# A ragged self-attention on one core: new step orders and PSUM banks for seven loops, and 64-row pairs in the two-tile loops

## The chip, the core and the metric

The kernel runs on one core of one Trainium2 chip. The metric is the device time of one execution in microseconds (us), as the median of several executions. Beside the timed executions one execution is recorded by the hardware profiler; its time is a little longer than the span of its trace, since some work lies around the first and the last instruction.

## What is computed

32 sequences of 64 to 511 rows (of 512 possible) and 512 columns in fp32 are each projected to queries, keys and values, attended with 8 heads of 64, and written back; rows beyond a sequence's length are zero.

```python
for b in range(batch):
    x_b = x[b, :lengths[b]]
    q, k, v = np.split(x_b @ w_qkv, 3, axis=-1)          # 512 x 1536 weights
    # reshape to 8 heads of 64
    scores = q @ k.T / sqrt(64)
    attn = softmax(scores)
    output[b, :lengths[b]] = attn @ v
```

The lengths are data. The program sorts the sequences by length on the chip.

## The kernel before

**Loops by length.** After sorting, the sequences are processed in 16 pairs, in order of falling length. `LOOPS` (line 220) holds twelve padded lengths N: 512, 448, 384, 352, 320, 288, 256, 224, 192, 160, 128 and 96. For each there is a loop whose body handles one pair in two *positions*, j = 0 and 1. A loop runs as often as the lengths ask; with this draw 1, 1, 1, 3, 1, 1, 1, 2, 1, 2, 1 and 1 times. A sequence of length N has n tiles of 128 rows: four for 512 and 448, three for 384 to 288, two for 256 to 160, one for 128 and 96. "Shared" loops (448, 320, 288, 192, 160) put the last half tiles of both sequences into one.

**What a position does.** In a position, the scores of sequence j are computed, exponentiated and multiplied with its values, while the queries, keys and values of the next sequence, o = 1 − j, are projected. So the projection in the last position of a loop is already for the first sequence of the next loop; the division of the results of a loop's last sequence is still running on VectorE when the next loop begins. The steps, which `position` (line 994) turns into instructions, are:

- S: scores (line 1174) of a group of heads, 64-row matmuls into two PSUM banks; ScalarE (ACT) exponentiates them from there (line 1192).
- A: attention times values (line 1336), 128-row matmuls of 65 columns into one bank; VectorE (DVE) takes the reciprocal of the sum (R, line 1348), multiplies in which rows live (U, line 1354), and divides into `out_nat` (O, line 1357).
- B: queries and keys of the next sequence as pairs of 64-row matmuls into two banks (`half_qk`, lines 1248 and 1222). The pair's two halves go to different banks at once; the second part, with the halves turned, adds the rest. U is the same for the values of two tiles (`half_values`, line 1267). The copies out of PSUM are lines 1255 and 1274.
- K and Q: the same by 128-row matmuls, one bank (`project`, line 275, copies at line 1294). V: values of one tile (line 286, copy at line 1310). W: values of a shared last tile (line 1128).
- L: a column of ones for rows that live (DVE, line 1093); P: the mask (DVE, line 1017) and the casts to fp16 (GpSimd, line 346); X: transposes of the next x by DMA on SyncE's queue (line 303); D: loading a later x, clearing tails, on the same queue.

**What sets the order.** `ORDER` (line 222) is a list of steps for each loop and position. "S0@67" is step S0 with banks 6 and 7. "B0a@50 ... B0b:da" is the first and the second part of B0; the second names the engines for its two copies, d for DVE and a for ACT. A star puts a copy on ACT. A loop whose list has no "@" gets its banks from `allotted` (line 959), a ring that gives the bank unused for longest. In the kernel before, 256, 224, 192, 160, 128 and 96 have no "@".

**Waits.** Each engine runs its instructions in the order of the list. Where an instruction needs a bank or buffer that another engine still holds, `plan_waits` (line 38) adds a semaphore wait. Loops can be entered from several others, so `by_rank` (line 1456) names every operation of a kind by how many of its kind follow in the position: O0 is the position's last division. A wait on a name is a wait on the operation of that rank, in whichever loop came before.

Of the kernel before, what the change touches and what calls it, by code (L numbers as in the profile page):

```python
# [162 lines left out]
def kernel(  # L163
# [25 lines left out]
    def ring(n, shape, dtype, name, pool=const):  # L189
# [804 lines left out]
    def position(N, j, at, ring):  # L994
# [213 lines left out]
        def halves(name, blocks, widths, copies, outs):  # L1208

            ks = ring.pop(0)

            def matmuls(turned):
                count = len(blocks[0])
                for m in range(count):
                    for c in range(NC):
                        for half in range(2):
                            z = half ^ turned
                            lhs, rhs = blocks[z][m]  # L1220
                            rows = slice(HD * half, HD * (half + 1))
                            last = nc.tensor.matmul(  # L1222
                                banks[ks[z]][:, m * widths : (m + 1) * widths],
                                lhs(rows, c),
                                rhs(rows, c),
                                start=(m == 0 and c == 0 and not turned),
                                stop=(c == NC - 1 and bool(turned)),
                            )
                return last

            held = (f"bk{ks[0]}", f"bk{ks[1]}")

            begun = ("b" if name[0] == "B" else "u") + name[1]

            def first():
                op(begun, "PE", lambda: matmuls(0), (f"xT{o}",), held)

            def second(engines):
                op(("q" if name[0] == "B" else "v") + name[1], "PE", lambda: matmuls(1), (f"xT{o}",), held, after=begun)
                for z in range(2):  # L1240
                    by_act, bank = engines[z] == "a", banks[ks[z]]
                    copy = lambda z=z, by_act=by_act, bank=bank: copies[z](copy_on(by_act), bank)
                    op(outs[z][0], "ACT" if by_act else "DVE", copy, (f"bk{ks[z]}",), outs[z][1])

            first()
            return second

        def half_qk(name, x):
# [5 lines left out]
            def into(buf):  # L1254
# [7 lines left out]
                (f"{up}{x}", tuple(f"{what}{o}.{x * gm + m}" for m in range(gm)))  # L1262
# [121 lines left out]
        for step in steps(N, j):  # L1384
            step = step.split("@")[0]
            kind, act = step[0], step.endswith("*")
            if kind in "BU":
                name, engines = step[:2], step[4:]
                if engines:
                    opened.pop(name)(engines)  # L1390
                else:
                    opened[name] = (half_qk if kind == "B" else half_values)(name, int(name[1]))
                continue
# [62 lines left out]
    def by_rank(ops):  # L1456


        kinds = {"bu": "b", "kqv": "g", "KQV": "G", "a": "a", "O": "O", "s": "s", "S": "S"}
# [249 lines left out]
```

## Time and profile before

| | us |
|---|---|
| median of 3 runs | 339.42 (339.03 to 340.7) |
| profiled execution | 340.88 |
| span of its trace | 339.0 |

| engine | busy us | share of the span |
|---|---|---|
| TensorE (PE) matmuls | 320.6 | 95% |
| ScalarE (ACT) | 260.4 | 77% |
| VectorE (DVE) | 213.8 | 63% |
| GpSimd (POOL) | 103.8 | 31% |

The loops begin, by their first matmul, at these times in the trace (us): 512 at 22.8, 448 at 60.2, 384 at 96.0, 352 at 121.4, 320 at 194.6, 288 at 217.1, 256 at 241.9, 224 at 257.1, 192 at 285.0, 160 at 298.2, 128 at 320.9, 96 at 327.6.

The busy share of an engine is a mean over all of these. The view that is used most is the timeline of one engine: each row has the start of a group of like instructions, the time from its first start to its last end, the engine, the line of the kernel, the operation, output and inputs, the shape, the count, and in brackets the idle time before it with what ended it. "<-issue" is idle time that ended with nothing the profile shows. The ends of matmuls are modelled, so rows of PE overlap by some tenths of a microsecond; the difference between the starts of two groups is the measure of what the first cost. Rows of the windows give the busy time of each engine in a stretch and the granted TensorE clock, 1.00 for full speed.

### The profile page before, as it was taken

The page shows a single profiled execution, that of the slowest core. Times are in us where ns is not written, and L with a number is a line of the kernel's source. Part 1 is how long each engine was busy: PE and PEld are TensorE (multiplying, and loading weights), DVE is VectorE, ACT ScalarE, POOL GpSimd, SP SyncE. Part 2 cuts the span into 40 slices and gives each one's busy share as a digit, 9 for nine tenths or more (in the row PEclk, how much of TensorE's full clock was granted, in tenths as well). Part 3 has the DMA queues.
Part 4 walks back from the last instruction along what each step waited for, and adds up shares of the span by engine and source line. Part 5 has one row for each costly group of instructions (what it writes and reads, how often), then busy time and mean ns, then how long its engine had stood idle before and what let it go on. Part 6 is the DMA issues. An engine that isn't in the chain of part 4 may idle for free.

```text
span 339.0 us, 12004 instructions
## 1 busy us (share of the span) xinstructions
PE 320.6 (95%) x4472; PEld 203.4 (60%) x4472; DVE 213.8 (63%) x675; ACT 260.4 (77%) x395; POOL 103.8 (31%) x149
## 2 busy tenths in 40 slices
PE   7989999899999989999999999799999999989891
PEld 5444536455556546556656656666668776868670
DVE  6555656676675556566475556657776665777774
ACT  5379899698968878978978898577667768877751
POOL 6546040504030330330232143043222224444231
PEclk9999999999999999999999999989999999999997
DMA  6974994463629957947948748979836865696771
GB/s 219 390 264 94 336 218 134 155 251 80 226 56 277 324 110 256 262 142 276 300 139 281 229 141 323 257 217 291 224 128 186 210 209 172 151 275 201 240 194 73
DMA packets 72127, 72.13 MB, mean 213 GB/s; under 512 B 41872, under 2 KB 41872, under 8 KB 72080
## 3 DMA queue, kind: packets, MB, share of 16 engines
q1 hardware_dynamic: 72032, 71.52, 70.5%
q8 instruction: 27, 0.44, 0.6%
q14 instruction: 20, 0.16, 0.2%
q10 hardware_dynamic: 48, 0.00, 0.0%
HBM read 28.32 MB, written 33.55 MB: 183 GB/s over the span
## 4 chain that ended last, share of the span: by engine, by line
PE 87%; DVE 5%; DMA 2%; issue 2%; ACT 1%; SPq 0%; POOL 0%; DVEq 0%; ACTq 0%; POOLq 0%
PE banks L1222 33%; PE banks L1336 15%; PE banks L1174 14%; PE banks L275 13%; PE banks L286 9%; DVE out_nat L1357 2%; PE banks L1128 2%; DMA x_nat<-in_x_dram 1%; DMA xT<-x 1%; DVE rcp L1354 1%; DVE rcp L1348 1%; PE banks L746 0%; ACT et L1192 0%; DVE kT L795 0%; SPq L623 0%
## 5 line engine op out<-in xcount | busy, mean ns | idle before, releaser
L1192 ACT ACTIVATE et<-banks 128x704 f16<-128x704 f32 (+7 forms) x260 | 201.6, 824 | 39.9 <-PE banks L1174 37.8
L346 POOL TENSOR_TENSOR x<-x_nat,mask 128x512 f16<-128x512 f32 x85 | 86.3, 1041 | 188.0 <-DVE mask L1017 158.9
L1222 PE MATMUL banks<-xT,w_r 64*128 64x352 f16 (+5 forms) x1024 | 102.5, 324 | 3.0 <-DVE out_nat L1357 3.0
L1174 PE MATMUL banks<-qz,kT 64*128 64x352 f16 (+11 forms) x640 | 76.5, 297 | 4.5 <-DVE out_nat L1357 1.4
L1336 PEld LDWEIGHTS banks<-v_aug,et 128*128 128x128 f16 x1792 | 62.0, 98 | 18.3 <-issue 8.3
L1222 PEld LDWEIGHTS banks<-xT,w_r 64*128 64x128 f16 x1024 | 47.1, 95 | 40.7 <-PE banks L1222 10.4
L1336 PE MATMUL banks<-v_aug,et 128*128 128x65 f16 x1792 | 69.2, 194 | 0.7 <-ACT et L1192 0.7
L1357 DVE TENSOR_TENSOR out_nat<-banks,rcp 128x256 f32<-128x256 f32 (+1 forms) x136 | 64.1, 471 | 5.4 <-DMA out_dram<-out_nat 0.8
L275 PE MATMUL banks<-xT,w_r 128*128 128x160 f16 (+6 forms) x512 | 51.4, 252 | 0.8 <-DMA xT<-x 0.5
L1174 PEld LDWEIGHTS banks<-qz,kT 64*128 64x128 f16 x640 | 27.6, 94 | 30.8 <-issue 8.0
L1255 DVE CAST qz<-banks 128x352 f16<-128x352 f32 (+5 forms) x41 | 22.6, 551 | 36.6 <-PE banks L1222 36.2
L275 PEld LDWEIGHTS banks<-xT,w_r 128*128 128x128 f16 x512 | 39.5, 98 | 7.4 <-issue 1.5
L286 PE MATMUL banks<-w_r,xT 128*128 128x512 f16 x156 | 39.3, 379 | 0.5 <-DVE xT L755 0.5
L1348 DVE RECIPROCAL rcp<-banks 128x4 f32<-128x4 f32 (+1 forms) x136 | 24.7, 181 | 19.6 <-PE banks L1336 18.3
L1222 PE MATMUL banks<-w_r,xT 64*128 64x512 f16 x256 | 33.0, 376 | 0.2 <-issue 0.2
L1274 DVE CAST v_aug<-banks 128x512 f16<-128x512 f32 x24 | 15.9, 690 | 17.5 <-PE banks L1222 17.5
L1255 DVE CAST kT<-banks 128x352 f16<-128x352 f32 (+5 forms) x41 | 22.1, 548 | 7.0 <-PE banks L1222 7.0
L1354 DVE TENSOR_TENSOR rcp<-rcp,v_aug 128x4 f32<-128x4 f32 (+1 forms) x108 | 20.4, 189 | 3.7
L1310 ACT CAST v_aug<-banks 128x512 f16<-128x512 f32 x21 | 12.5, 595 | 11.0 <-PE banks L286 11.0
L286 PEld LDWEIGHTS banks<-w_r,xT 128*128 128x128 f16 x156 | 12.9, 97 | 13.2 <-ACT et L1192 1.1
L1222 PEld LDWEIGHTS banks<-w_r,xT 64*128 64x128 f16 x256 | 12.2, 94 | 10.6 <-PE banks L1222 1.0
L1294 ACT CAST kT<-banks 128x320 f16<-128x320 f32 (+3 forms) x17 | 8.4, 491 | 7.2 <-PE banks L275 7.2
(91 smaller groups left out, 154.3 us busy)
## 6 DMA issues: line engine op xcount, KB each, us to landing
x_nat<-in_x_dram SPq DMA_DIRECT2D x12, 768.0 KB, 5.4
out_dram<-out_nat SPq DMA_DIRECT2D x12, 768.0 KB, 4.0
x_nat<-in_x_dram SPq DMA_DIRECT2D x14, 512.0 KB, 3.9
x_nat<-in_x_dram SPq DMA_DIRECT2D x7, 1024.0 KB, 6.6
out_dram<-zeros SPq DMA_DIRECT2D x12, 512.0 KB, 5.4
out_dram<-out_nat SPq DMA_DIRECT2D x12, 512.0 KB, 4.4
out_dram<-out_nat SPq DMA_DIRECT2D x4, 1024.0 KB, 4.6
out_dram<-zeros SPq DMA_DIRECT2D x12, 256.0 KB, 5.4
```

Source lines behind the costliest of these rows:

```text
L275: last = nc.tensor.matmul(dst[:, 0:N], w_r[:, c, w0 : w0 + P], xT[:, c, 0:N], start=(c == 0), stop=(c == NC - 1),)
L286: last = nc.tensor.matmul(pv, xT[:, c, t * P : (t + 1) * P], w_r[:, c, 2 * D : 3 * D], start=(c == 0), stop=(c == NC - 1),)
L346: return engine.tensor_tensor(out=x16, in0=x32, in1=live.broadcast_to([P, D]), op=ALU.mult)
L1174: last = nc.tensor.matmul(psc[par][:, x * wide : x * wide + N], kT[r, i, c0 : c0 + P], qz[r, i, 0:N], start=True, stop=True,)
L1192: return nc.scalar.activation(out=et[:, :, x0:x1, 0:N], in_=got.rearrange("p j (x q) -> p j x q", q=wide)[:, :, x0:x1, 0:N], func=AF.Exp, ...
L1222: last = nc.tensor.matmul(banks[ks[z]][:, m * widths : (m + 1) * widths], lhs(rows, c), rhs(rows, c), start=(m == 0 and c == 0 and not tur ...
L1255: return lambda copy, bank: copy(out=buf[:, ms, 0:N], in_=bank[:, 0 : gm * N].rearrange("p (m q) -> p m q", q=N),)
L1274: return lambda copy, bank: copy(out=v_bufs[o][:, t, :, 0:HD], in_=bank.rearrange("p (h d) -> p h d", d=HD))
L1336: last = nc.tensor.matmul(pav[:, g, qt, :], e_bufs[e][:, c0 + qt * P : c0 + (qt + 1) * P], v_aug[:, kt, h, :], start=(kt == 0), stop=(kt = ...
L1348: return nc.vector.reciprocal(out=rcp, in_=pav[:, :, :, HD])
L1354: return nc.vector.tensor_tensor(out=rcp, in0=rcp, in1=rows, op=ALU.mult)
L1357: return nc.vector.tensor_tensor(out=o_t[:, 0:n, h0 * HD : (h0 + heads) * HD].rearrange("p t (g d) -> p g t d", d=HD), in0=pav[:, :, :, 0:HD],
```

## The change

`ORDER` has new lists for 512, 384, 352, 320, 256, 224 and 192, of which 352's differ in a few banks and in the order of four steps; the lists of 448, 288, 160, 128 and 96 are the same. In 256, 224 and 192, banks are now written out, and 128-row K, Q (and in 256 and 224 V) steps are replaced by 64-row pairs. For that `halves` can place two blocks of the output in each of its two banks. Where two blocks go to a bank (N up to 256), the work of a B is in three parts, a, b and c: block 0 of both banks with the halves straight; block 0 with the halves turned and block 1 turned; block 1 straight. The copies, one for each bank with both blocks, follow the last part. Each part waits for the part before it. The names of first and middle parts now carry the kind, number and part, and `by_rank` files the u parts with the other last ones. A queries' or keys' copy of two blocks is `into` as before with a width of 2N. 

```diff
     ORDER = {
-        512: "L P D S0@67 U1a@34 S1@01 S2@67 U1b:dd S3@12 B0a@50 S4@67 B0b:da S5@23 B3a@14 S6@67 B2a@05 S7@23 "
-        "B2b:dd S8@67 B3b:ad A0@0 S9@23 S10@67 A1@5 A2@4 A3@1 S11@23 U0a@05 S12@67 U0b:dd S13@34 A4@1 "
-        "S14@67 B1a@20 S15@45 B1b:aa A5@6 A6@5 X A7@3 | L P D S0@12 U1a@47 S1@56 U1b:da S2@12 B3a@30 "
-        "S3@45 B3b:dd S4@12 U0a@76 S5@45 U0b:dd S6@01 B1a@23 S7@45 B1b:ad S8@67 S9@01 A0@4 B2a@23 S10@67 "
-        "B2b:dd S11@45 B0a@10 S12@67 B0b:dd S13@45 S14@23 A1@6 A2@7 S15@45 A3@1 A4@3 A5@0 A6@2 X A7@5",
+        512: "L P D S0@56 S1@23 U1a@74 S2@56 U1b:dd S3@01 B1a@32 S4@67 B1b:dd S5@45 S6@01 A0@6 A1@3 S7@45 "
+        "B0a@27 S8@01 B0b:dd S9@34 B2a@65 S10@12 B2b:ad U0a@74 S11@23 S12@56 U0b:ad S13@01 A2@3 A3@2 A4@4 "
+        "S14@56 B3a@37 S15@12 B3b:ad A5@4 A6@5 X A7@7 | L P D S0@23 U0a@10 S1@56 U0b:ad S2@23 U1a@47 "
+        "S3@01 B1a@56 S4@23 B1b:da S5@01 U1b:dd S6@23 B2a@56 S7@01 B2b:ad S8@34 B3a@72 S9@01 A0@5 A1@6 "
+        "S10@34 B3b:dd S11@01 S12@56 A2@3 A3@4 S13@12 B0a@07 S14@56 A4@3 S15@12 B0b:da A5@3 A6@1 X A7@0",
         448: "L P D S0@67 B2a@32 S1@45 B2b:da S2@67 B1a@10 S3@23 B1b:dd S4@67 B0a@54 S5@23 B0b:dd S6@01 S7@67 "
...
-        384: "L P D U0a@32 S0@45 S1@67 U0b:dd S2@01 B1a@54 S3@67 B1b:dd S4@23 B2a@10 S5@67 B2b:dd S6@23 S7@45 "
-        "A0@6 A2@7 S8@01 B3a@32 S9@56 B3b:aa B0a@10 S10@45 B0b:ad S11@23 V2*@6 A4@0 X A6@2 | L P D S0@67 "
-        "B3a@43 S1@01 B3b:dd S2@67 B2a@52 S3@01 B2b:dd S4@34 S5@67 V2@1 A0@2 S6@45 B1a@73 S7@01 B1b:aa "
-        "A2@2 S8@01 S9@45 U0a@67 B0a@32 S10@01 S11@45 B0b:da U0b:da A4@0 X A6@1",
-        352: "L P D V2@4 S0@56 S1@01 U0a@27 S2@56 S3@34 U0b:dd S4@01 B2a@65 S5@34 B2b:dd S6@01 A0@2 A2@7 S7@01 "
-        "B0a@56 S8@34 B0b:ad B1a@10 S9@34 B3a@27 S10@56 B1b:dd S11@34 B3b:aa A4@6 X A6@3 | L P D S0@01 "
-        "B2a@42 S1@67 B2b:da S2@01 B0a@53 S3@67 B1a@42 S4@01 B1b:dd S5@67 B0b:ad S6@01 A0@4 S7@67 U0a@25 "
-        "S8@01 S9@34 U0b:ad B3a@10 S10@67 S11@34 B3b:aa A2@5 A4@7 A6@3 V2*@6 X",
-        320: "L P D S0@45 U0a@10 S1@67 S2@45 U0b:da B1a@76 S3@45 B1b:ad S4@23 A0@0 S5@45 B0a@67 S6@23 B0b:ad "
-        "S7@45 B3a@10 S8@67 B3b:da S9@45 B2a@32 S10@67 S11@01 B2b:da A2@5 A4@4 X A6@7 | L P S0@23 S1@01 "
-        "W0@6 D B0a@32 S2@01 B0b:da S3@45 B2a@76 S4@01 S5@23 B2b:dd U0a@45 S6@01 S7@23 U0b:da B1a@76 "
-        "S8@01 B3a@32 S9@45 B1b:da B3b:dd S10@01 S11@45 A0@7 A2@6 A4@3 X A6@2",
+        384: "L P D S0@56 B3a@34 S1@12 B3b:ad S2@56 B2a@07 S3@23 B1a@14 S4@56 B2b:ad S5@23 B1b:dd S6@56 B0a@70 "
+        "S7@12 B0b:dd S8@34 U0a@65 S9@12 S10@34 U0b:ad S11@12 A0@0 A2@7 A4@6 V2*@3 X A6@0 | L P D S0@12 "
+        "B1a@47 S1@56 B1b:ad S2@01 B2a@32 S3@56 B3a@74 S4@01 B2b:da S5@56 B3b:da U0a@03 S6@12 S7@67 "
+        "U0b:da B0a@54 S8@12 S9@67 A0@0 A2@3 S10@12 B0b:da S11@67 A4@0 V2*@2 X A6@7",
+        352: "L P D V2@4 S0@56 S1@01 U0a@27 S2@56 S3@34 U0b:dd S4@01 B2a@65 S5@34 B2b:dd S6@01 A0@7 A2@2 S7@01 "
+        "B0a@56 S8@34 B0b:aa B1a@10 S9@34 B3a@27 S10@56 B1b:dd S11@34 B3b:aa A4@6 X A6@3 | L P D S0@01 "
+        "B0a@42 S1@67 B0b:da S2@01 B2a@53 S3@67 B1a@42 S4@01 B1b:dd S5@67 B2b:ad S6@01 A0@4 S7@67 U0a@25 "
+        "S8@01 S9@34 U0b:ad B3a@10 S10@67 S11@34 B3b:aa A2@5 A4@7 V2*@6 X A6@3",
+        320: "L P D S0@12 B2a@45 S1@67 B2b:ad S2@23 U0a@01 S3@67 S4@45 U0b:da B0a@67 S5@34 B1a@25 S6@01 B0b:dd "
+        "S7@34 B1b:ad S8@01 A0@6 S9@23 B3a@57 S10@01 B3b:dd S11@23 A2@4 A4@6 X A6@5 | L P S0@23 S1@01 "
+        "W0@4 D B1a@76 S2@01 B2a@32 B1b:ad S3@01 B2b:dd S4@45 A0@6 S5@01 B0a@73 B3a@24 S6@01 B0b:dd S7@56 "
+        "B3b:ad A2@1 S8@67 S9@23 U0a@54 S10@67 S11@01 U0b:da A4@3 X A6@0",
         288: "L P D S0@45 B2a@72 B3a@36 S1@45 B2b:da B3b:dd S2@45 S3@01 U0a@27 S4@56 S5@34 U0b:dd S6@01 B0a@56 "
...
-        256: "L P V0 V1 S0 S1 K2 Q0 S2 S3 A0 K0* A2 A4 Q2* X D A6",
-        224: "L P K0 K2* S0 S1 Q0* Q2 S2 S3 A0 A2 V1* A4 V0* X D A6",
-        192: "L P V0* S0 S1 Q0 K0* S2 S3 A0 K2* A2 A4 Q2* X D A6 | L P K0* S0 S1 W0 V0 S2 S3 A0 Q0* A2 A4 K2* "
-        "Q2* X D A6",
+        256: "L P U0a@23 S0@45 U0b:da B1a@10 S1@67 B0a@54 S2@23 B0b S3@67 B1b B0c:aa A0@3 A2@2 A4@7 A6@6 "
+        "B1c:aa X D | L P U0a@34 S0@12 U0b:ad B0a@05 S1@67 B1a@21 B0b S2@34 S3@67 B0c:da B1b A0@3 B1c:aa "
+        "X D A2@4 A4@7 A6@6",
+        224: "L P B0a@30 S0@12 B0b B1a@54 B0c:da S1@67 B1b S2@01 U0a@23 S3@67 B1c:dd U0b:aa X D A0@1 A2@0 A4@7 "
+        "A6@4 | L P B1a@65 S0@23 B1b B0a@01 B1c:ad B0b S1@23 S2@67 B0c:dd U0a@45 A0@3 A2@0 S3@12 U0b:aa X "
+        "D A4@7 A6@6",
+        192: "L P B1a@01 B0a@23 S0@45 B1b S1@67 B0b B1c:da S2@45 B0c:dd S3@67 A0@1 V0*@0 X D A2@2 A4@3 A6@5 | "
+        "L P W0@4 B0a@60 S0@12 B0b B1a@37 B0c:dd S1@12 B1b S2@45 A0@6 S3@12 B1c:aa A2@0 A4@5 V0*@4 X D "
+        "A6@6",
         160: "L P S0 S1 S2 K0 Q2* A0 Q0* A2 K2* A4 V0* X D A6 | L P S0 S1 S2 W0 Q0 K0* A0 Q2* A2 K2* A4 V0* X "
...
-        def halves(name, blocks, widths, copies, outs):
+        def halves(name, blocks, width, copies, outs):
...
-            def matmuls(turned):
-                count = len(blocks[0])
-                for m in range(count):
+            def matmuls(parts):
+                for m, turned, opens in parts:
                     for c in range(NC):
...
-                                start=(m == 0 and c == 0 and not turned),
-                                stop=(c == NC - 1 and bool(turned)),
+                                start=(c == 0 and opens),
+                                stop=(c == NC - 1 and not opens),
...
+            todo = [[(0, 0, True)], [(0, 1, False)]]
+            if len(blocks[0]) == 2:
+                todo[1].append((1, 1, True))
+                todo.append([(1, 0, False)])
+            begun = []
+            def go_on(engines):
+                k, parts = len(begun), todo[len(begun)]
+                last = k == len(todo) - 1
+                title = "qu"[name[0] == "U"] + name[1] if last else f"b{'BU'.index(name[0])}{name[1]}{k}"
+                op(title, "PE", lambda: matmuls(parts), (f"xT{o}",), held, after=begun[-1] if begun else "")
+                begun.append(title)
+                for z in range(2 if last else 0):
...
+            return go_on
...
-        kinds = {"bu": "b", "kqv": "g", "KQV": "G", "a": "a", "O": "O", "s": "s", "S": "S"}
+        kinds = {"b": "b", "kqvu": "g", "KQV": "G", "a": "a", "O": "O", "s": "s", "S": "S"}
```

More of the change, by code (lines that the diff above doesn't have):

```diff
@@ L1222, in matmuls @@
                             last = nc.tensor.matmul(
-                                banks[ks[z]][:, m * widths : (m + 1) * widths],
+                                banks[ks[z]][:, m * width : (m + 1) * width],
                                 lhs(rows, c),
                                 rhs(rows, c),
-                                start=(m == 0 and c == 0 and not turned),
-                                stop=(c == NC - 1 and bool(turned)),
+                                start=(c == 0 and opens),
+                                stop=(c == NC - 1 and not opens),
                             )
@@ L1231, in halves @@
             held = (f"bk{ks[0]}", f"bk{ks[1]}")
[L1233 to L1240, printed above, removed]
+            todo = [[(0, 0, True)], [(0, 1, False)]]
[7 more added lines that the diff above has]
+                title = "qu"[name[0] == "U"] + name[1] if last else f"b{'BU'.index(name[0])}{name[1]}{k}"
+                op(
+                    title,
+                    "PE",
+                    lambda: matmuls(parts),
+                    (f"xT{o}",),
+                    held,
+                    after=begun[-1] if begun else "",
+                )
+                begun.append(title)
+                for z in range(2 if last else 0):
                     by_act, bank = engines[z] == "a", banks[ks[z]]
@@ L1243, in second @@
                     op(outs[z][0], "ACT" if by_act else "DVE", copy, (f"bk{ks[z]}",), outs[z][1])
-            first()
-            return second
+            return go_on
         def half_qk(name, x):
@@ L1261, in half_qk @@
             outs = [
-                (f"{up}{x}", tuple(f"{what}{o}.{x * gm + m}" for m in range(gm)))
+                (f"{up}{x * gm}", tuple(f"{what}{o}.{x * gm + m}" for m in range(gm)))
                 for up, what in (("Q", "qz"), ("K", "kT"))
@@ L1388, in position @@
                 name, engines = step[:2], step[4:]
-                if engines:
-                    opened.pop(name)(engines)
-                else:
+                if name not in opened:
                     opened[name] = (half_qk if kind == "B" else half_values)(name, int(name[1]))
+                opened[name](engines)
                 continue
```

## The prediction

> **What bounds the kernel now.** I read the page first, then TensorE's timeline for places where it stood idle, then VectorE's timeline at the same places.
>
> ```profile
> span 339.0 us, 12004 instructions
> ...
> PE 320.6 (95%) x4472; PEld 203.4 (60%) x4472; DVE 213.8 (63%) x675; ACT 260.4 (77%) x395; POOL 103.8 (31%) x149
> ...
> PE 87%; DVE 5%; DMA 2%; issue 2%; ACT 1%; SPq 0%; POOL 0%; DVEq 0%; ACTq 0%; POOLq 0%
> ```
>
> TensorE is busy for 95% of the span and carries 87% of the chain of waits. The change removes no matmul work, so it can gain only what PE loses: its idle time, its slowed time, and its changes between 64-row and 128-row matmuls. The rows below are PE's timeline at the borders ("seams") between loops, and within loop 352; the bracket is idle time and its releaser.
>
> ```profile
> 60.20 0.36 PE L1174 MATMUL banks<-qz,kT 64*128 64x448 f16 x2
> 61.80 0.74 PE L1222 MATMUL banks<-xT,w_r 64*128 64x448 f16 x6 [1.23 <-DVE out_nat L1357]
> ...
> 96.02 1.04 PE L1222 MATMUL banks<-w_r,xT 64*128 64x512 f16 x8 [0.22 <-issue]
> ...
> 121.42 1.03 PE L286 MATMUL banks<-w_r,xT 128*128 128x512 f16 x4
> 122.38 0.32 PE L1174 MATMUL banks<-qz,kT 64*128 64x352 f16 x2
> 122.98 0.32 PE L1174 MATMUL banks<-qz,kT 64*128 64x352 f16 x2 [0.27 <-DVE out_nat L1357]
> 123.14 1.03 PE L1222 MATMUL banks<-w_r,xT 64*128 64x512 f16 x8
> 124.00 0.31 PE L1174 MATMUL banks<-qz,kT 64*128 64x352 f16 x2
> 125.05 0.32 PE L1174 MATMUL banks<-qz,kT 64*128 64x352 f16 x2 [0.74 <-DVE v_aug L1310]
> ...
> 195.63 0.70 PE L1174 MATMUL banks<-qz,kT 64*128 64x320 f16 x4
> 196.17 0.60 PE L1222 MATMUL banks<-w_r,xT 64*128 64x512 f16 x4
> ...
> 217.13 0.30 PE L1174 MATMUL banks<-qz,kT 64*128 64x288 f16 x2
> 219.24 2.10 PE L1222 MATMUL banks<-xT,w_r 64*128 64x288 f16 x16 [1.81 <-DVE out_nat L1357]
> 221.11 0.47 PE L1174 MATMUL banks<-qz,kT 64*128 64x288 f16 x2
> 221.35 1.78 PE L1222 MATMUL banks<-xT,w_r 64*128 64x288 f16 x16
> ...
> 296.70 0.41 PE L1336 MATMUL banks<-v_aug,et 128*128 128x65 f16 x8
> 298.19 0.73 PE L1174 MATMUL banks<-qz,kT 64*128 64x160 f16 x16 [1.08 <-ACT qz L1294]
> ```
>
> VectorE at the same seams, with the clock of the fourth (the window's columns: length; PE, PEld, DVE, ACT, POOL busy; granted clock; DMA share; GB/s):
>
> ```profile
> 61.23 0.42 DVE L1357 TENSOR_TENSOR out_nat<-banks,rcp 128x256 f32<-128x256 f32 x1
> ...
> 124.07 0.26 DVE L1093 TENSOR_SCALAR v_aug<-alive 128x24 f16 x1 [1.15 <-issue]
> ...
> 124.31 0.68 DVE L1310 CAST v_aug<-banks 128x512 f16<-128x512 f32 x1
> ...
> 218.54 0.56 DVE L1357 TENSOR_TENSOR out_nat<-banks,rcp 128x384 f32<-128x384 f32 x1
> 220.43 0.20 DVE L1093 TENSOR_SCALAR v_aug<-alive 128x16 f16 x1 [1.33 <-issue]
> ...
> 297.56 0.42 DVE L1357 TENSOR_TENSOR out_nat<-banks,rcp 128x256 f32<-128x256 f32 x1
> ...
> 219.24:222.60 3.36, 3.36 (x30) 2.45 (x32) 0.50 (x4) 0.67 (x2) 1.61 (x2) 0.50 1.20 281
> ```
>
> Three things are to be seen. First, a new loop's first projection waits for a bank whose last division (L1357) is still queued on DVE: PE starts at 61.80, 0.15 us after the division that ends at 61.65, and at 219.24, 0.14 us after 219.10. That 0.15 is the release latency. Second, on entering loops 352 and 288 DVE stands for 1.15 and 1.33 us "<-issue" at the first instruction of the new code (L1093), with nothing to wait for. The V copy at 124.31 is late by that, and S3 at 125.05 by the copy. Third, after 1.81 us of idle PE runs at half clock until 222.6.
>
> **The change, part by part.** Against the profiled execution: 340.88 us, the 339.0 of its span and 1.9 around it.
>
> *320 to 288.* Old: 320 ends with A6@2 and 288 begins with S0, B2a@72, so B2a waits for the very last division. From 217.13 two S matmuls take 0.12 (sixteen of that width take 0.98, below), so B2a is 1.99 late. The slowed stretch is 3.36 us at half clock, so 1.7 more is lost: 3.7 in all. New: 320 ends with S11@01 U0b:da A4@3 X A6@0. B2a@72 needs the exps of S9 and S10, B3a@36 the division of A4 and an exp: all before A6's. What is late next: S0@45 needs both V copies of U0b (one 0.69 on DVE, one 0.6 on ACT), with A4 and A6 (18 AV matmuls each, 1.1 us in all) between, and I take 0.25. S3@01 needs A6's division, which has the two B parts (about 2 us) to hide in. U0a@27 needs Q2's copy, which stands on DVE behind L and M, hence behind the 1.33 us entry stall if it stays: I take 1.0. The instruction stream of DVE keeps its length within 0.3% (770 for 772), so I let both stalls stay. −3.7 + 0.25 + 1.0 = **−2.4**; −3.5 if the stall goes.
>
> *512 to 448.* Old: S0, B2a@32 with bank 2 held by the last but one division. 61.80 − 60.20, less 0.20 for two matmuls (0.16 at 352 columns, 122.98 to 123.14), is 1.40 lost. New: 512 ends A5@3 A6@1 X A7@0, so B2a needs the last but two, a whole A6 and A7 earlier. Its Q2 copy is then behind L and M on DVE, in front of S3@23: I take 0.2 for that. **−1.2**.
>
> *384 to 352.* Lost: 122.98 − 122.38 less 0.15, and 125.05 − 124.00 less 0.15: 1.35. New: 384 ends V2*@2 X A6@7 instead of A4@0 X A6@1. S1@01 now needs exps and A4; that is 0.45 gained. The 0.9 at S3@34 hangs on the V2@4 copy behind the stall, and the steps of 352 there are unchanged. **−0.45**; −1.3 if the stall goes, 0 if another bank binds.
>
> *192 to 160.* S0 of 160 waits for the last division: 298.19 − 296.70, less 0.24 for eight AV matmuls (269.69 to 269.93, below), is 1.25, of which 0.1 is the row change below. 160 keeps its own banks, and 192's written-out ones change what its first two held last. Then S2 waits for V0's ACT copy and K0 for A6: I take 0.45. **−0.8**.
>
> *Three small seams* (448 to 384, 352 to 320, 288 to 256). The rows at 96.02 (0.22) and 195.63 (0.54 until 196.17 for four S, where twice 0.16 would do even at 352 columns) show two; I take the third, which shows no idle row, at half of one. **−0.55**.
>
> *Row changes and parts.* A switch between 64 and 128 rows, and the cost of a second part:
>
> ```profile
> 268.83 1.03 PE L286 MATMUL banks<-w_r,xT 128*128 128x512 f16 x4
> 269.69 0.41 PE L1336 MATMUL banks<-v_aug,et 128*128 128x65 f16 x8
> 269.93 0.38 PE L286 MATMUL banks<-w_r,xT 128*128 128x512 f16 x1
> ...
> 153.02 0.32 PE L1174 MATMUL banks<-qz,kT 64*128 64x352 f16 x2
> 153.18 0.76 PE L1222 MATMUL banks<-xT,w_r 64*128 64x352 f16 x8
> 153.78 0.31 PE L1174 MATMUL banks<-qz,kT 64*128 64x352 f16 x2
> 154.00 1.37 PE L1222 MATMUL banks<-xT,w_r 64*128 64x352 f16 x16
> ...
> 233.01 1.14 PE L1222 MATMUL banks<-xT,w_r 64*128 64x288 f16 x16
> 233.99 0.28 PE L1174 MATMUL banks<-qz,kT 64*128 64x288 f16 x2
> ```
>
> Four 128-row matmuls of 512 take 0.86 (268.83 to 269.69), with a switch to 64 rows after them 0.96 (121.42 to 122.38), and eight 64-row ones 0.86 (123.14 to 124.00). So a pair costs what one 128-row matmul does, and a **switch costs 0.10**. A second part one S behind its first starts 0.22 after the S (153.78 to 154.00) instead of 0.16 (153.02 to 153.18): 0.06 for each such place. Counted along the steps, 384 loses 4 switches and 4 such places: **−0.65**. 320 gains 4 switches, loses 2 places, and puts more copies on ACT in between, which I take at 0.2: **+0.4**. The eight positions' pairs in 256, 224 and 192 are narrower than any that the trace has; at 288 columns sixteen matmuls, eight pairs, take 0.98 (233.01 to 233.99), 122.5 ns a pair, where 288/512 of 215 would be 121. Some 320 pairs at 0 to 1.5 ns more: I take +0.3. They lose 8 switches (−0.8) and gain 4 places where a part waits (+0.2). **−0.3** for the three together.
>
> *Rank names and copies at 256, 224, 192.* A wait names an operation by its rank from the end of a position, so 224's B0a@30 on entry waits for 256's A2 division too, and its first S for the copies after part c; 192's S0@45 waits for V1's copy on ACT. The nearest row to each wait is one ACT copy (0.595, below) and its bounds are 0 and that plus 0.15. I take **+0.5** for both.
>
> ```profile
> 22.80:60.20 37.40, 37.36 (x512) 19.40 (x513) 21.28 (x62) 33.88 (x38) 12.83 (x14) 1.00 0.72 196
> ...
> 241.90:257.13 15.23, 15.14 (x177) 10.74 (x178) 11.98 (x37) 9.60 (x12) 4.29 (x5) 1.00 0.57 153
> ...
> L1192 ACT ACTIVATE et<-banks 128x1024 f16<-128x1024 f32 x40 | 39.1, 1031 | 8.6 <-PE banks L1174 8.0
> ...
> L1274 ACT CAST v_aug<-banks 128x512 f16<-128x512 f32 x8 | 4.8, 595 | 0.0
> ```
>
> *512 itself.* ACT is busy 33.88 of 37.40 us. The new order has four copies on ACT in its second position where the old has two (and three for four in the first): 16 × 1.03 + 4 × 0.595 = 18.9 of 18.7 us, so an S may wait for a late exp. Bounds 0 and one copy, 0.6; I take **+0.4**.
>
> X and D (SP's transposes and loads) move by one A or two at most and no wait names SP at these seams, so I cost them at nothing; their cover is the whole position, and 0.2 would be lost where it is gone.
>
> Sum: −2.4 −1.2 −0.45 −0.8 −0.55 −0.65 +0.4 −0.3 +0.5 +0.4 = **−5.05**. Profiled: 335.8. The median shown is 1.46 below the profiled execution, so the forecast is **334.4 us**; the bounds of the single terms put it between 332.3 and 336.5.
>
> One rule speaks against the new pairs. The Trainium skill, "TensorEngine Tiling (Array Packing)", section "Gotcha 1: PSUM Pressure", says that different row tiles write to different PSUM banks. Here a B of a two-tile loop holds two banks through three parts, where a 128-row projection held one; no row of this trace has three parts.
>
> **Rivals.**
> 1. *Copies bunch in the two-tile loops, and it gets slower.* Nothing is copied until part c; then two blocks wide copies come at once ("B0c:aa", "B1c:aa"). In the first position of 256 ACT would have four exps and five copies: 4 × 1.03 + 5 × 0.595 = 7.1 of 7.6 us (half of 15.23). If each of the eight positions of 256, 224 and 192 waits 1 us for such copies, 334.4 + 8 = **342.4**. It decides from 0.84 us a position (6.7 us brings 341.1). For it: 256's ACT, 9.60 busy now. Against it: two to four A or S steps stand between most parts c and the S that needs them.
> 2. *The entry stalls go.* They are unexplained "issue" time; if the new code lands otherwise, S3 of 352 and U0a of 288 wait no more: −0.9 and −1.1, and the smaller terms fall with them (−0.9): **331.5**.
> 3. *The gain is half given back.* Of the waits above, several end in the next one (S3 of 448, S0 of 288, S2 of 160) for longer than I took: half the 5 us, **337**.
> 4. *The clock halves anyway.* Idles of 1.23 (61.80), 1.08 (298.19) and 0.74 did not halve it; 1.81 did. A 1.0 us wait at U0a of 288 with 0.25 just before it may: +1.7, **336.1**. The Trainium skill, "TensorE: Matmul & The Clock Gate", Part 1, puts the fall at one idle window of about 3.4 us; the trace disagrees, since 1.81 us was enough here. By that rule the half clock would have another cause than this wait and would stay: the same 336.1.
> 5. *It doesn't do what it says*: rank names hold the old waits at the seams, and only the inner orders change: −0.3, **339.1**.
>
> **How the numbers follow.** Forecast 0.50, rival 1 0.11, 2 0.14, 3 0.12, 4 0.07, 5 0.06. A measurement of this kernel can tell 0.5%, 1.7 us: faster is below 337.7, slower above 341.1. Faster: 0.50 + 0.14 + 0.07 and two thirds of rival 3, 0.79. Slower: most of rival 1, 0.10. Same: 0.11. The range reaches to rivals 2, 3, 4 and 5 and leaves out rival 1 and the far half of 2: 330.8 to 339.4.
>
> **What would show it.** At 288's entry PE's idle should fall from 1.81 to about 1 or less, and no window there should show a clock of 0.50; B2a of 448 should come within 0.3 us of S0; S0 of 160 should not wait for a division. Wrong if the loop of 256 gets longer than its 15.23 by more than 0.5 us, with S waiting for copies, or if new idles behind ACT copies appear in 512 and 320.

## The result, and the profile after

The changed kernel takes **337.59 us** (median of 6, 337.0 to 337.73); the kernel before, run with it, 339.92. The ratio is 0.9929, with a 95% interval of 0.9908 to 0.9951: faster by 0.7%, 2.3 us. Forecast was 334.4, 5.05 us less than the kernel before. The direction was right, the size was not.

The page after, the rows that answer to those of before:

```profile
span 335.7 us, 12603 instructions
...
PE 318.0 (95%) x4776; PEld 203.5 (61%) x4776; DVE 211.9 (63%) x673; ACT 262.5 (78%) x397; POOL 103.7 (31%) x149
...
PE 85%; DVE 5%; issue 3%; SPq 2%; DMA 2%; ACT 1%; POOL 0%; DVEq 0%; POOLq 0%
```

PE is the bound as before. New on the chain are 2% of SP's queue; "issue" has 3% for 2%. PE's timeline after, at the places that the prediction named and at those that it did not (start, length, line, shape, idle before and its releaser):

```profile
59.98 0.36 PE L1179 MATMUL banks<-qz,kT 64*128 64x448 f16 x2
60.18 0.92 PE L1228 MATMUL banks<-xT,w_r 64*128 64x448 f16 x8
...
122.51 0.32 PE L1179 MATMUL banks<-qz,kT 64*128 64x352 f16 x2 [0.80 <-DVE v_aug L1326]
...
214.91 0.30 PE L1179 MATMUL banks<-qz,kT 64*128 64x288 f16 x2 [0.18 <-issue]
215.04 1.16 PE L1228 MATMUL banks<-xT,w_r 64*128 64x288 f16 x16
...
218.37 0.82 PE L1228 MATMUL banks<-w_r,xT 64*128 64x512 f16 x6 [0.83 <-DVE qz L1271]
...
241.90 0.61 PE L1228 MATMUL banks<-xT,w_r 64*128 64x256 f16 x8 [0.79 <-issue]
...
253.52 0.56 PE L1228 MATMUL banks<-xT,w_r 64*128 64x224 f16 x8 [0.45 <-DVE out_nat L1373]
...
267.66 0.56 PE L1228 MATMUL banks<-xT,w_r 64*128 64x224 f16 x8 [0.27 <-ACT v_aug L1290]
...
281.91 0.84 PE L1228 MATMUL banks<-xT,w_r 64*128 64x192 f16 x16 [0.39 <-issue]
...
293.76 0.82 PE L1179 MATMUL banks<-qz,kT 64*128 64x160 f16 x16
294.90 0.80 PE L280 MATMUL banks<-xT,w_r 128*128 128x160 f16 x9 [0.32 <-DVE out_nat L1373]
```

At 448 (59.98 to 60.18) and at 288 (214.91 to 215.04) the first projection follows its S without a wait, and U0a of 288 waits 0.83 for Q2's copy. In 256 PE stands for 0.79 with no releaser, in the middle of one step; at the borders of 224 and inside it stand waits of 0.27 to 0.45. VectorE's rows show why some stay:

```profile
121.53 0.26 DVE L1098 TENSOR_SCALAR v_aug<-alive 128x24 f16 x1 [1.30 <-issue]
...
217.39 0.20 DVE L1098 TENSOR_SCALAR v_aug<-alive 128x16 f16 x1 [1.29 <-issue]
...
327.57 0.42 DVE L1373 TENSOR_TENSOR out_nat<-banks,rcp 128x256 f32<-128x256 f32 x1 [1.15 <-DMA out_dram<-out_nat]
```

Both entry stalls of DVE are still there (1.30 and 1.29), and at 327.57 a division waits 1.15 us for a store: that is new.

The loops, from the first matmul of each to the first of the next, worked out from PE's timelines. "again" is a second profiled execution of the same kernel, from the experiments; the two columns on the right are experiments too.

| us | before | before again | after | after again | old 256, 224, 192 | old 256, 224 |
|---|---|---|---|---|---|---|
| 512 | 37.40 | 37.40 | 37.52 | 37.32 | 37.59 | 37.36 |
| 448 | 35.81 | 35.88 | 34.36 | 34.36 | 34.36 | 34.37 |
| 384 | 25.40 | 25.43 | 24.90 | 24.89 | 24.89 | 24.90 |
| 352 and 320 | 95.72 | 95.69 | 95.67 | 95.72 | 95.61 | 95.73 |
| 288 | 24.76 | 23.14 | 22.29 | 22.24 | 22.12 | 22.03 |
| 256 | 15.23 | 15.21 | 16.31 | 15.88 | 15.32 | 15.17 |
| 224 | 27.83 | 27.83 | 28.39 | 28.36 | 27.83 | 27.92 |
| 192 | 13.24 | 13.23 | 11.85 | 12.00 | 13.23 | 12.27 |
| 160 | 22.70 | 22.70 | 23.17 | 23.48 | 22.69 | 23.18 |
| 128 | 6.69 | 6.68 | 6.69 | 6.69 | 6.69 | 6.69 |
| 96 to the end | 11.45 | 10.98 | 12.10 | 12.54 | 10.99 | 11.12 |
| span | 339.0 | 337.1 | 335.7 | 336.0 | 334.3 | 333.7 |

### The profile page after: what moved, and what is told of

It reads as the page before. It is cut to its first block, busy times and chain, and to the rows that moved or that the text cites. A ratio compares the mean times of both kernels' runs of the same rounds, so it can differ in the third digit from the quotient of the medians.

```text
span 335.7 us, 12603 instructions
## 1 busy us (share of the span) xinstructions
PE 318.0 (95%) x4776; PEld 203.5 (61%) x4776; DVE 211.9 (63%) x673; ACT 262.5 (78%) x397; POOL 103.7 (31%) x149
## 4 chain that ended last, share of the span: by engine, by line
PE 85%; DVE 5%; issue 3%; SPq 2%; DMA 2%; ACT 1%; POOL 0%; DVEq 0%; POOLq 0%
PE banks L1228 43%; PE banks L1352 16%; PE banks L1179 14%; PE banks L291 6%; PE banks L280 4%; PE banks L1133 2%; DVE out_nat L1373 2%; DMA out_dram<-out_nat 1%; DVE rcp L1370 1%; DMA x_nat<-in_x_dram 1%; SPq L308 1%; DVE rcp L1364 1%; SPq L1069 1%; PE banks L751 1%; DVE kT L800 0%
## 5 line engine op out<-in xcount | busy, mean ns | idle before, releaser
L1228 PE MATMUL banks<-xT,w_r 64*128 64x352 f16 (+8 forms) x1536 | 130.7, 299 | 1.9 <-issue 1.2
L1228 PEld LDWEIGHTS banks<-xT,w_r 64*128 64x128 f16 x1536 | 70.0, 94 | 40.2 <-PE banks L1228 9.1
L1271 DVE CAST qz<-banks 128x448 f16<-128x448 f32 (+5 forms) x49 | 27.5, 565 | 40.6 <-PE banks L1228 40.4
L1228 PE MATMUL banks<-w_r,xT 64*128 64x512 f16 x352 | 45.3, 376 | 1.0 <-DVE qz L1271 0.8
L1271 DVE CAST kT<-banks 128x448 f16<-128x448 f32 (+5 forms) x50 | 27.2, 553 | 8.0 <-PE banks L1228 7.9
L291 PE MATMUL banks<-w_r,xT 128*128 128x512 f16 x108 | 27.7, 379 | 0.6 <-DVE xT L760 0.5
L280 PE MATMUL banks<-xT,w_r 128*128 128x160 f16 (+3 forms) x256 | 23.5, 244 | 0.5 <-DVE out_nat L1373 0.5
L280 PEld LDWEIGHTS banks<-xT,w_r 128*128 128x128 f16 x256 | 16.9, 98 | 5.2 <-DVE out_nat L1373 0.9
L1271 ACT CAST qz<-banks 128x352 f16<-128x352 f32 (+5 forms) x31 | 15.0, 482 | 2.6 <-PE banks L1228 2.5
L1271 ACT CAST kT<-banks 128x352 f16<-128x352 f32 (+4 forms) x30 | 15.0, 499 | 1.5 <-PE banks L1228 1.5
```

The source lines that it names most:

```text
L280: last = nc.tensor.matmul(dst[:, 0:N], w_r[:, c, w0 : w0 + P], xT[:, c, 0:N], start=(c == 0), stop=(c == NC - 1),)
L291: last = nc.tensor.matmul(pv, xT[:, c, t * P : (t + 1) * P], w_r[:, c, 2 * D : 3 * D], start=(c == 0), stop=(c == NC - 1),)
L1228: last = nc.tensor.matmul(banks[ks[z]][:, m * width : (m + 1) * width], lhs(rows, c), rhs(rows, c), start=(c == 0 and opens), stop=(c == N ...
L1271: return lambda copy, bank: copy(out=buf[:, ms, 0:N], in_=bank[:, 0 : gm * N].rearrange("p (m q) -> p m q", q=N),)
```

## The experiments

Two theories at first. Theory 1: the seams gave what was forecast, and 256 to 160 and the end give back 2 us. Theory 2: the pairs pay, and the other seams gave less. Ratios below are to the kernel before, run on the same chip, with 95% intervals. The kernels are the changed one or the one before with lists of `ORDER` exchanged, unless a diff says otherwise.

**The kernel before again.** No edit.

> The kernel before, unchanged, to see its own scatter: its six executions lie at 339.0 to 339.4 and at 340.4 to 340.7. If the half clock at 288's entry comes in some executions and not in others, the times fall in two groups about 1.3 us apart and the granted clock of the longer ones is lower by about 0.005; if the scatter has another cause (transfers, code loading), times and clock have no relation.

Measured: 339.75 (0.9999, 0.9981 to 1.0018). In its profile 288 takes 23.14 us, not 24.76: PE waits 1.81 us at B2a as before, and the clock is not halved.

```profile
219.44 1.16 PE L1222 MATMUL banks<-xT,w_r 64*128 64x288 f16 x16 [1.81 <-DVE out_nat L1357]
220.41 0.30 PE L1174 MATMUL banks<-qz,kT 64*128 64x288 f16 x2
...
219.50:222.90 3.40, 3.40 (x50) 2.42 (x49) 1.76 (x6) 1.99 (x4) 1.72 (x2) 1.00 1.26 276
```

Here 16 matmuls take 0.97 us where the first profile has 1.87, and the window's clock is 1.00 where that had 0.50. Over the 113 executions of the kernel before in all the experiments' jobs, 43 have a granted clock of 0.991 or less, with a median of 340.96 us and none under 340.27; the 70 others have a median of 339.34, but reach 341.3. The first profile, with the half clock, has a mean clock of 0.989, the second 0.995. So the half clock comes in about four executions of ten and costs 1.6 us; the profile of before was one of them. The count is approximate: every profile also ends at half clock, and that part of the mean varies too.

What decides between the two profiles can be read from them. The recorded changes of the clock lie whole multiples of 3.41 us apart (219.21, 222.62 and 335.26 us in the first profile). Counted back from a change, the first profile has the whole idle time in one stretch of 3.41 us, the second has it across two (its last change is at 333.93, 33 such stretches behind 221.29; the bound before that is 217.88, in the middle of the idle time). The two stretches, first profile and second (length, then PE's busy time; the granted clock is third from the end):

```profile
215.80:219.21 3.41, 1.52 (x43) 1.22 (x39) 3.05 (x11) 0.78 (x2) 0.00 (x0) 1.00 0.95 280
```

```profile
217.88:221.29 3.41, 1.85 (x31) 1.73 (x33) 1.87 (x8) 0.97 (x2) 0.11 (x1) 1.00 1.10 264
```

With PE busy for 1.52 us the clock is halved for the next stretch, with 1.85 it is not.

**One list alone.** 320's, and 512's, in the kernel before:

```diff
     ORDER = {
-        320: "L P D S0@45 U0a@10 S1@67 S2@45 ... A0@7 A2@6 A4@3 X A6@2",
+        320: "L P D S0@12 B2a@45 S1@67 B2b:ad ... U0b:da A4@3 X A6@0",
```

> The kernel before with only the new list of 320. Both theories: PE's wait of 1.8 us at B2a of 288 and the half clock after it go, a wait of about 0.9 at U0a for Q2's copy comes; loop 288 takes 22.3 for 24.8 us, 320 the same 22.5. The time is 2.4 below before, 337.5, if nothing behind takes it back; 1.8 below, if the end of the kernel (stores on SP's queue) gives back 0.6 as in the changed kernel.

Measured: 339.05 (0.9974, 0.9955 to 0.9992), 0.9 us by the ratio, less than the 1.8 or 2.4 expected. 288 takes 22.07; 320 itself 22.97 for 22.51, the +0.4 of the prediction. The granted clock is 0.992 or more in all 12 executions: the half clock is gone. Against an execution of before without half clock that is only 0.8 us of span (336.3 for 337.1).

> The kernel before with only the new list of 512. Theory 1: 448 takes 34.4 for 35.8 us, its 1.4 us at B2a gone, 512 itself 37.4 to 37.6, and the time is 1.2 to 1.4 below before. Rival: ACT's fuller second position in 512 gives back 0.4 and more, 512 at 37.8, and the time is 0.9 below or less. The half clock at 288's entry comes in about half of the executions, as before.

Measured: 339.04 (0.9967, 0.9944 to 0.999). 448 takes 34.46, 512 37.32: 1.4 us gained, and ACT gives nothing back. The half clock is still there in 7 of its 12 executions.

**One digit.**

```diff
-        "S8@01 B3a@32 S9@45 B1b:da B3b:dd S10@01 S11@45 A0@7 A2@6 A4@3 X A6@2",
+        "S8@01 B3a@32 S9@45 B1b:da B3b:dd S10@01 S11@45 A0@7 A2@6 A4@3 X A6@0",
```

> The kernel before with one digit changed: the last AV of 320 goes to bank 0 (A6@0 for A6@2), so that 288's B2a@72 waits for no last division. Theory 1 (that one bank is the whole seam): PE's idle of 1.8 us at 288's entry goes, a wait of about 1 us for Q2's copy behind DVE's entry stall takes its place, 288 takes 22.1 for 23.1 us (24.8 in the executions with the half clock), 320 keeps 23.5. No execution has a half clock there, so the granted clock is 0.994 or more in nearly all, and the median is 1.0 + 0.75 below before's, about 1.7. Theory 2 (the rest of 320's new list is needed): B3a@36 takes over the wait, and the time is that of before.

Measured: 339.47 (0.9991, 0.9966 to 1.0017). In time that is theory 2, in the trace neither of the two: B2a of 288 waits no more, B3a waits 0.38 (218.90), and the clock stays full, so 288 takes 22.95. But a wait comes at 320's own entry, and 320 takes 23.11 for 22.51:

```profile
195.61 1.04 PE L1222 MATMUL banks<-w_r,xT 64*128 64x512 f16 x8 [0.69 <-DVE out_nat L1357]
...
218.90 0.67 PE L1222 MATMUL banks<-xT,w_r 64*128 64x288 f16 x8 [0.38 <-issue]
...
222.00 0.39 PE L1222 MATMUL banks<-w_r,xT 64*128 64x512 f16 x2 [1.09 <-DVE qz L1255]
```

U0a@10 at 195.61 needs bank 0, which the last AV of 320 now holds, and the wait is on the rank "last division": on entry that is 352's last division, which held another bank. This is what the prediction says of rank names, and why one list is not free of the others.

**The pairs.**

```diff
-        256: "L P U0a@23 S0@45 U0b:da ...",
-        224: "L P B0a@30 S0@12 B0b ...",
-        192: "L P B1a@01 B0a@23 S0@45 B1b ...",
+        256: "L P V0 V1 S0 S1 K2 Q0 S2 S3 A0 K0* A2 A4 Q2* X D A6",
+        224: "L P K0 K2* S0 S1 Q0* Q2 S2 S3 A0 A2 V1* A4 V0* X D A6",
+        192: "L P V0* S0 S1 Q0 K0* S2 S3 A0 ...",
```

> The changed kernel with the lists of before (128-row projections, automatic banks) in 256, 224 and 192. Theory 1 (the gain of the seams is given back in 256 and 224 by waits and by one stall of PE's own instructions): the four loops 256 to 160 go back from 79.7 to 79.0 us, the time is 0.5 to 1.0 below the changed kernel, about 336.9. Theory 2 (the pairs pay, and the forecast was too high at the other seams): 1 us or more above it, 338.6.

Measured: 336.56 (0.9909, 0.9886 to 0.9932), 1 us below the changed kernel by the medians; the two intervals overlap. The waits of 256 and 224 go, 192 goes back to 13.23, and 96 to the end falls to 10.99. The time is that of theory 1, the place is not: 256 to 160 take 79.07 here, 79.0 to 79.7 in the four profiles of the changed kernel (two of them from the section below) and 79.0 in the kernel before. What differs in all four is the end, by 0.8 to 1.5 us.

> The kernel before with only the new lists of 256, 224 and 192 (64-row pairs). Theory 1: 0.7 slower than before, 340.6, with a PE stall without a releaser of about 1 us in 256 if the pairs bring it; if the stall hangs on where the code lies, it is absent or elsewhere and the time is that of before less 0.2. Theory 2: 1 us faster than before.

Measured: 341.07 (1.0016, 0.9992 to 1.0041), no gain. 256 takes 15.35, 224 28.40, 192 11.85, 160 23.18: against before 0.14 and 0.57 lost, 1.38 gained, 0.48 lost. No PE stall in 256. Theory 2 falls. The profile has the half clock at 288, and its first matmul of 512 comes at 23.73 for 22.80, where nothing was changed.

> The changed kernel with the lists of before in 256 and 224 alone; 192 keeps its pairs. By loops: 256 15.3, 224 27.8, 192 11.9 and 160 23.2 (192's last division no longer holds 160's first bank). Theory 1 (the pairs of 256 and 224 only cost; the gain of 192 is its seam): 0.9 below the kernel with all three old, 335.7. Theory 2 (the gain of 192 needs 224's new end): 192 takes 13.2 or its wait moves to its entry, and the time is that of all three old, 336.6.

Measured: 336.4 (0.9907, 0.9875 to 0.9939). By loops 192 takes 12.27 for 13.23, 160 takes 23.18 for 22.69: the seam's 1 us comes without 224's new end, and 160 gives half of it back. In time it is the same as with all three old, and it has the lowest median of all runs.

> The changed kernel with the list of before in 224 alone. Theory 1 (224's waits at its entry, between its iterations and at its exit cost 0.55, and so does no other loop's): 224 27.9 for 28.4. It tells also which list brings DVE's wait of about 1 us for a store at the end, seen in four of four executions of the changed order: if it is 224's, 96 and what follows go from 12.1 to 11.0 us and the time is 1.6 below the changed kernel; if not, 0.5 below.

Measured: 337.46 (0.9931, 0.9908 to 0.9954), the same as the changed kernel. 224 takes 27.92, 0.45 less; but 192 takes 12.82 (its V copy is late), and 96 to the end 11.56. So it is not 224's list alone that makes DVE wait for a store: it waits 0.86 here, for the store before the one of the changed kernel.

> New lists in 512, 384, 352 and 192; 256 and 224 as before; 320 as before but with A6@0. It differs from the kernel with old 256 and 224 only in 320's list. If 320's list brings nothing beyond the one bank: the same time, 336.3 (352 and 320 together 95.5 to 95.7 us); if its inner order pays: 0.4 slower, 336.8; if it costs, as where it was changed alone (23.9 for 23.5): 0.3 faster, 336.0.

Measured: 338.18 (0.995, 0.9927 to 0.9972), 1.8 above old 256 and 224, and dearer than all three forecasts. By loops 320's whole list is worth 1.7 beside 384's and 352's: with A6@0 alone 352 and 320 take 96.5 for 95.7, and 288 22.93 for 22.03. Another 0.8 of this profile is no gain of 320's list: 96 to the end takes 11.93 for 11.12, with a wait of 1.22 us for a store.

**The stall in 256 and the end.**

> The changed kernel, unchanged. Theory A (PE's stall of 0.97 us in the middle of B0b of 256 comes from where the code lies): it is there again, at the same instruction, and 256 takes 16.3 us; theory B (it is chance of one execution): it is gone and 256 takes 15.3. The 1.1 us that DVE waited for a store at the end is there again if stores are late by the order of the kernel, gone (96 and what follows 11.0 us) if it was chance. Granted clocks of 0.992 and more in most executions, since the idle that halved it is down to 0.8 us.

Measured: 337.71 (0.9926, 0.9899 to 0.9953). The stall in the middle of B0b is gone, yet 256 takes 15.88: PE now loses 0.5 us at U0a of the second position, and this time the row names a releaser, SyncE's queue, on which the transposes of the next x came late (the last one landed at 244.75):

```profile
244.89 1.04 PE L1228 MATMUL banks<-w_r,xT 64*128 64x512 f16 x8 [0.35 <-SPq L325]
```

DVE's wait for the store is there again, 1.58.

> The changed kernel with 64 register moves more at the head of PE's program, where PE waits for data anyway; all of PE's later code lies 64 instructions further on. Theory A: the stall in 256 goes or comes at another matmul, with 256 at 15.3 and the time 1 us below the changed kernel, or the same if it only moves. Theory B: no relation to the shift.

> The same with 128 register moves. Theory A: as with 64, the stall gone or at another matmul. Theory B: no relation.

Measured: 337.37 (0.9921, 0.989 to 0.9952) and 337.67 (0.9935, 0.9908 to 0.9963). Both profiles have the 12603 instructions of the changed kernel: the register moves are not in them, and both are the changed kernel once more. As such they tell something: 256 takes 15.35 in both, as in six of the seven other kernels with 256's pairs (15.54 in the one with old 224). So the stall without a releaser came in one of eleven profiles with that list, and its cause stays open. DVE waits for the store in all four profiles of the changed kernel (0.84 to 1.58), with 96 to the end at 11.8 to 12.5.

In these four a load of 16 KB on queue 8, which carries PE's instructions, starts while that store is on its way; in the profiles whose end takes 11.0 us it falls elsewhere, or on a store for which DVE waits 0.25 us at most. To move it, increments of a semaphore that nobody reads were put into PE's program (`nc.tensor.sem_inc`), 24 or 64 ahead of loop 128, or 96 at the head:

> The changed kernel with 24 semaphore increments (of a semaphore that nobody reads) more in PE's program just ahead of loop 128, where PE waits 1.1 us for a division anyway. In all executions of the changed order a load of PE's instructions (16 KB on queue 8) starts between 0.8 and 1.9 us after the beginning of loop 96, while the store whose last packets come 1 us late is under way; where that load lies elsewhere, no store is late. Theory F (the load of code delays the store): the load comes 0.5 to 0.8 us earlier, DVE's wait for the store shrinks or goes and what follows the start of 96 takes 11.0 to 11.6 for 12.1 us, or it stays if 24 are too few. Rival (the store is slow by itself): the load moves, the wait stays.

> The same with 64 increments. Theory F: the load of code lies ahead of 96's first store, DVE does not wait for the store, 96 and what follows take 11.0 us; PE may start 128 up to 1.3 us later where the increments last longer than its wait, and the time is 1.1 below the changed kernel less that. Rival: the wait of about 1 us stays.

> The changed kernel with 96 such increments at the head of PE's program; all its later code lies 96 instructions further on, and each load of 16 KB (256 instructions) comes some 4 us earlier against the work. Theory F: the store at the end is not late and 96 with what follows takes 11.0 us. For the stall of PE in 256, which came with 0.97 and 0.52 us in two executions of the changed order and not at all in two more: a place of its own if it hangs on the code's layout, none if it is chance.

Measured: 340.84 (1.0018, 1.0 to 1.0036), 346.86 (1.0186, 1.0158 to 1.0214) and 352.62 (1.0355, 1.0329 to 1.0381). Each increment cost PE about 0.15 us, so the work moved too. With 24 the load starts 1.0 us after 96's start and DVE waits 1.42; with 64 it starts ahead of 96, no store is waited for, and the last part takes 10.97; with 96 the last part takes 11.75, with a wait of 1.05 for an earlier store, during which the load now lies. In line with theory F, but not clean.

So the last two put instructions there that PE skips:

```diff
+            if N == 128:
+                with nc.tensor.If_lt(of(pair, "PE"), 0):
+                    for k in range(64):
+                        nc.tensor.sem_inc(shift, 1)
+                nc.tensor.end_ifs()
             body, after = f"loop_{N}", f"after_{N}"
```

> The changed kernel with 64 instructions that PE skips by one branch, ahead of loop 128, where it waits 1.1 us anyway. Nothing more is executed than a compare and a branch, but the code behind lies 64 instructions further on, so that the load of PE's code in loop 96 (0.8 to 1.9 us after 96's start) comes some 2 us earlier against the work, unless the branch itself sets off a load. Theory F (that load delays the store): DVE's wait for the store goes, 96 and what follows 11.0 for 12.1 us, the time 336.5 for 337.6. Rival (the store is late by itself): 12.1 and 337.6 again.

> The same with 128 skipped instructions: the load comes some 4 us earlier, in loop 128. Theory F: as with 64, 336.5. Rival: 337.6.

Measured: 336.83 (0.9911, 0.9882 to 0.9939) and 336.77 (0.9918, 0.9891 to 0.9945), 0.5 to 0.9 below the four medians of the changed kernel. The intervals of all of these overlap, so the times alone do not show it; the traces have to. The DMA view of the changed kernel, from 324 to 327.8 us, and the same view with 64 skipped, from 324.4 to 327 (last row: number and size of the stores, and the median of their times to landing):

```profile
q1 hardware_dynamic: 288, 0.52, 36.3%
q8 instruction: 1, 0.02, 2.6%
...
out_dram<-out_nat SPq DMA_DIRECT2D x2, 256.0 KB, 3.3
```

```profile
q1 hardware_dynamic: 275, 0.50, 50.2%
...
out_dram<-out_nat SPq DMA_DIRECT2D x1, 256.0 KB, 2.0
```

With the load beside them the two stores take 3.3 us by their median, without it this one takes 2.0. DVE's division at that place then does not wait:

```profile
325.91 0.49 DVE L1370 TENSOR_TENSOR rcp<-rcp,v_aug 128x4 f32<-128x4 f32 x1
326.44 0.42 DVE L1373 TENSOR_TENSOR out_nat<-banks,rcp 128x256 f32<-128x256 f32 x1
```

With 128 skipped the load falls on the store before, and a wait of 1.16 us stands at that one, so 96 to the end is 11.9 there and 11.2 with 64. (160 took 24.15 in the run with 64, 1 us more than elsewhere, with longer waits for GpSimd and DVE; that was not followed up.) The rival falls, since the late store moves with the load. Theory F holds over all runs: in nine profiles DVE waits 0.84 us or more for a store shortly before or in loop 96, and in each of the nine a load on queue 8 starts while that store is on its way. (In loop 160 DVE waits 0.5 us or more for a store in every profile, before and after, with no such load; that is another matter.) The forecast of 336.5 for both does not hold in this way: with 128 the wait only moved. What sets the load's place within the program was not tried further.

## Why the prediction was wrong, point by point

- **320 to 288, and the base.** The mechanism held: the wait of 1.81 us and the half clock go, S0 waits 0.18 (I took 0.25), U0a 0.83 (I took 1.0) behind a DVE stall that stayed. Against the profiled execution even the size is right: 24.76 to 22.29 is 2.47 for the 2.4 forecast. The step that failed is the last one, "The median shown is 1.46 below the profiled execution", together with "so 1.7 more is lost: 3.7 in all". The half clock was taken as part of the kernel; it comes in 43 of 113 executions, 0.6 us on the mean. Its 1.7 us were taken off in the sum, and then 1.46 us once more to go from the profiled execution to the median: that difference is the half clock (1.62 between the two profiles of before), so I counted it twice. Against the median 288's gain is 0.85 and those 0.6.
- **512 to 448**, **384** and the small seam between: 1.45 in 448 and 0.5 in 384, for 1.2 + 0.2 and 0.65: right.
- **352 and 320.** S1 of 352 waits no more, S3 still 0.80: right. Together the two loops stay at 95.7, where −0.3 was forecast.
- **192 to 160.** 192 is 1.1 to 1.4 shorter, 160 0.5 to 0.9 longer (K0 waits for the division instead of S0): 0.5 to 0.9 net for 0.8. The prediction's row names an ACT copy as the releaser of S0 and not the division; that copy ends at 297.38, the division at 297.98 and S0 starts at 298.19, so the division is the likelier one.
- **256, 224, 192.** The pairs' stream costs nothing that can be seen (256 15.35 for 15.21), and their rows' switches gain nothing either. The "+0.5 for both" of rank names and copies is 0.55 in 224 alone. In 256 the stall of 1 us in one profile was in no term, and the 0.5 us of another, a wait for SyncE's transposes, falls under "X and D", which I costed at nothing. So 256 did get longer by more than the 0.5 us that the prediction gave as a sign of being wrong, but no S waits for copies: between 236 and 294 us PE waits for ACT's copies 0.3 us in all, and rival 1 is out.
- **512's ACT**, +0.4: did not come (37.32 to 37.52 for 37.40).
- **The end.** I costed nothing there; DVE's wait for a store takes 1.1 us (96 to the end 11.8 to 12.5 for 11.0). I costed what the lists move, not where the program's loads fall.

By sizes, from the mean of the four profiles of the changed kernel and with the half clock at its mean: about 1.0 of the 2.7 us is the half clock, 1.0 the two-tile loops with 160, 1.2 the end, 0.3 in 352 and 320. Some 0.7 went the other way, 0.4 of it in 512; most of the rest lies ahead of 512, whose start varies from 22.5 to 23.7 us between profiles that have the same program up to there, and is luck.

Rival 3 gave the nearest time (337), mostly by luck: only U0a's and K0's waits are gains that ended in the next wait, and the rest is the base and the end, which it does not name. Rival 4 was wrong: no profile of the changed kernel has a half clock ahead of its end. In Part 1 of "TensorE: Matmul & The Clock Gate" the Trainium skill speaks of a free-running window of activity. That fits what these executions show, where one and the same idle of 1.81 us halves the clock in some and not in others. The Trainium skill puts the fall there at a whole idle window of about 3.4 us. That does not fit: 1.81 us was enough where it lay in one stretch. Rival 5's rank names did hold a wait, in the one-digit kernel.

## What to carry to other kernels

A single profile shows one draw of what varies between executions: before a loss is put into a sum, compare the executions' granted clocks, and take the profiled execution's own group as the base. A change to an engine's program can move its instruction loads onto a transfer that something waits for, far behind the edit. Where waits are named by rank, one bank changed at a loop's end is waited for at that loop's own entry too.

## What the runs showed of the hardware

- The half clock follows a stretch of 3.41 us in which PE was busy for about half of the time or less. In the 19 profiles, laid on the grid of their recorded clock changes, every stretch at full clock behind the first 30 us with PE busy for 1.77 us or less was followed by half clock, and none with 1.85 or more. The ends of matmuls are modelled, so the bound between the two is no finer than that.
- The half clock lasts 3.41 us or a multiple: 3.41 after an idle of 1.81 us at 288, 6.83 after PE stood for 3.1 us, 10.24 after 9.2 us (the last in the run with 64 increments, whose window of 10.15 us within it shows a clock of 0.50):

```profile
320.25:330.40 10.15, 5.70 (x52) 4.66 (x52) 1.86 (x7) 1.67 (x3) 0.00 (x0) 0.50 0.16 58
```

- DVE's stall at the entry of loops 352 and 288 was 1.15 to 1.33 us in both profiles of before and all four of after; it does not vary as the half clock does. What it waits for stays open.
- A store of 256 KB took 2.0 us at its shortest, and up to 4.3 us where a load of 16 KB on queue 8 started during it.
- PE took about 0.15 us for each semaphore increment put in by itself (96 of them made the start 15 us later).
